# Gathering the attention products of a tile into one place of the matmul stream, in two PSUM banks used in turn, in a hybrid attention and pooling block

## The chip, the cores and the metric

The kernel runs on one core of one Trainium2 chip. The metric is device time in microseconds (us) of one execution, as the median of several runs. PE is TensorE, DVE is VectorE, ACT is ScalarE, POOL is GpSimd and SP is the sync engine, whose queue issues all DMAs here.

## The reference

One decoder block on x of 2048 x 1024 in fp32, with a final RMSNorm. What matters here is the attention: three groups of 8 heads of 64, with windows 128, 512 and 2048 and dilations 1, 4 and 16. Their outputs are joined by a softmax over the groups' log-denominators.

```python
proj = h @ w_in[l]                      # (2048, 8192): q, k, v of 3 groups, then gates and pooling
for gi, (win, dil) in enumerate(ATTN_GROUPS):
    o, lse = dilated_window_attention(qkv[:, :, gi, 0], qkv[:, :, gi, 1], qkv[:, :, gi, 2], dil, win // dil, bias_g)
    outs.append(o); lses.append(lse)
wts = jax.nn.softmax(jnp.stack(lses, axis=0), axis=0)
attn = jnp.sum(wts[..., None] * jnp.stack(outs, axis=0), axis=0)
y_attn = (attn * jax.nn.silu(z_attn)) @ w_attn_br[l]
```

A query attends to the 129 keys of its window (the queries' own block of 128 and the block before it). The pooling branch, the gates and the output projection follow.

## The kernel before, in words

The sequence is worked in two halves `h` of 1024 positions. In each half the projections run first in 12 units: four head pairs `hp` times three groups `g`, in the order 1, 2, 0. A unit (`unit`, L531) projects K, Q and V of one head pair, each in 8 main steps. A main step (`mm3`, L245) is six matmuls of 128x512: high and low parts of weights and activations, three products, two halves. So a unit has 24 main steps. Weights are split into a high part by VectorE (L217) and a low part by GpSimd (L218), six buffers deep.

The attention of one unit is a generator (`attention`, L545) that runs beside the main steps of the next unit: `weave` (L130) takes the main generator step by step and after each step advances the attention as often as keeps it even, `n_side` advances over `n_main - skip` steps. The last attention of a half runs beside the four pooling projections, 32 main steps (L976). PE and SP carry out their instructions in the order in which the program writes them (the manual schedule of L965); the other three engines are ordered by the scheduler.

One attention has 8 tiles of 128 queries. For a tile `t`:

- `prefetch` (L556): for tiles at the edge of the second half, DMAs of the keys of the first half and of this tile's keys into `khist`, and of the values into `vhist`.
- `logits` (L589): six matmuls with 64 rows into two banks `qk`; VectorE adds the bias and takes the minimum (L616), ScalarE takes the exponential (L620), VectorE adds the two blocks and takes a dot product with the identity (L629, L631).
- `transposed` (L638): two transposes into the bank `tp`; ScalarE copies them to `pT` (L646). For a tile with 256 keys GpSimd then multiplies and subtracts (L649, L650).
- `output` (L655): two or four matmuls into the bank `ops` (each is two in the trace); VectorE writes the row (L669 or L672). Groups 1 and 2 store it, group 0 reads the stored rows of the others and weighs all three (L683 to L701).
- `joined` (L703), group 0 only: one transpose of the joined row into `tp`; ScalarE copies it to `attnT` (L706).
- `flip` (L573), twice per attention: four transposes of V into `tp`, copied by ScalarE to `v` (L579).

PSUM has eight banks: four for the projections, two `qk`, one `tp`, one `ops`. Every one of the pieces above ends with a `yield`, so that a main step can stand between any two of them. The loop that sets their order is the end of `attention`:

```python
for s in range(12):
    if s < 8:
        prefetch(s + 2); logits(s); yield
    if s < 2:
        flip(s); yield
    if 1 <= s < 9:
        transposed(s - 1); yield
    if 2 <= s < 10:
        output(s - 2); yield
    if g == 0 and 4 <= s:
        joined(s - 4); yield
```

## Time and profile before

| what | value |
|---|---|
| median of 3 runs (lowest to highest) | 2363.19 us (2361.03 to 2369.22) |
| profiled execution, and its span | 2364.48 us, 2362.6 us |
| PE busy with matmuls | 2207.8 us (93%) in 11786 instructions |
| VectorE, ScalarE, GpSimd busy | 46%, 25%, 41% of the span |
| six products of the projections L253 (6000 matmuls, three groups) | 675.8 + 627.0 + 623.9 us |
| chain that ended last, by engine | PE 18%, no other over 2% |

The span is what the profiler saw of the program; the execution's own time is 1.9 us longer. A group of rows names a line, an engine, the tile written and the tiles read, the count, the busy time and the mean of one. A wait is given with the engine and line that released it. The granted clock is 1.00 for PE at 2.4 GHz and 0.50 at 1.2 GHz. Matmuls overlap: the time one takes of PE is read from start to start, not from its own length.

### The profile page before, as it was taken

Reading aid. Unit: us, or ns where it says so; the run is one execution under the profiler, and the core shown is the slowest. Engines: PE = TensorE matmul, PEld = TensorE weight load, DVE = VectorE, ACT = ScalarE, POOL = GpSimd, SP = SyncE. Lnnn points to the kernel's source line nnn. Section 1 sums busy time; section 2 is a strip of 40 time slices with the busy share of each in tenths; the row PEclk is TensorE's granted clock in tenths of the full one; section 3 lists DMA queues with packets and bytes.
Section 4 is the critical chain, followed back from the end, with each engine's and each line's share of the span. In section 5 each row is a group of like instructions: output and inputs, shape, how many; then the busy total and the mean of one; then the engine's idle time right before and its main releaser. Section 6 shows DMA issues by size and latency. Waiting matters only on the chain. (4 is left out here: it accounts for less than half of the span.)

```text
span 2362.6 us, 32338 instructions
## 1 busy us (share of the span) xinstructions
PE 2207.8 (93%) x11786; PEld 1802.4 (76%) x11786; DVE 1081.4 (46%) x3048; ACT 596.7 (25%) x1554; POOL 966.2 (41%) x930
## 2 busy tenths in 40 slices
PE   4799999999999999999899989999999899999998
PEld 3577777777777888888877767767777678888898
DVE  5444536336367211115764475564664861111155
ACT  4223232233332101102433333223322320010023
POOL 3322323213245223446754344344443552244365
PEclk7899999999999999999999999999999999999999
DMA  7243222222221112114432322222223111121134
GB/s 261 97 145 90 73 68 64 81 61 70 82 64 47 45 54 72 55 53 152 170 103 74 99 69 71 85 72 85 66 80 91 54 54 45 49 86 45 54 125 152
DMA packets 142685, 198.56 MB, mean 84 GB/s; under 512 B 13542, under 2 KB 109983, under 8 KB 142528
## 3 DMA queue, kind: packets, MB, share of 16 engines
q1 hardware_dynamic: 142528, 196.51, 26.2%
q8 instruction: 93, 1.52, 0.3%
q14 instruction: 64, 0.52, 0.1%
HBM read 157.62 MB, written 35.16 MB: 82 GB/s over the span
## 5 line engine op out<-in xcount | busy, mean ns | idle before, releaser
L218 POOL TENSOR_TENSOR wlo<-wraw,whi 128x512 fp32r<-128x512 f32 x352 | 470.7, 1340 | 848.9 <-PE mm L253 410.9
L253 PE MATMUL mm<-hhi,whi 128*128 128x512 f32 x2000 | 675.8, 419 | 2.0 <-DVE klo L509 2.0
L253 PE MATMUL mm<-hlo,whi 128*128 128x512 f32 x2000 | 627.0, 395 | 0.0
L253 PE MATMUL mm<-hhi,wlo 128*128 128x512 f32 x2000 | 623.9, 393 | 0.0
L217 DVE CAST whi<-wraw 128x512 fp32r<-128x512 f32 x352 | 197.5, 566 | 582.2 <-PE mm L253 411.4
L253 PEld LDWEIGHTS mm<-hhi,wlo 128*128 128x128 f32 x2000 | 378.3, 189 | 86.1
L253 PEld LDWEIGHTS mm<-hlo,whi 128*128 128x128 f32 x2000 | 378.3, 189 | 85.0
L253 PEld LDWEIGHTS mm<-hhi,whi 128*128 128x128 f32 x2000 | 338.6, 191 | 56.5 <-issue 3.0
L620 ACT ACTIVATE l<-l,row 128x256 f32<-128x256 f32 (+1 forms) x384 | 181.4, 474 | 493.1 <-DVE row L616 362.4
L616 DVE CUSTOM_DVE_ANT_0 l<-qk,bias 128x256 f32<-128x256 f32 (+1 forms) x384 | 133.7, 383 | 297.5 <-PE qk L613 275.3
L649 POOL TENSOR_TENSOR pT<-pT,prevm 128x256 f32<-128x256 f32 x140 | 100.2, 716 | 267.5 <-ACT pT L646 266.2
L734 ACT ACTIVATE sg<-mm 128x1024 f32<-128x1024 f32 x48 | 49.4, 1028 | 554.9 <-PE mm L253 422.5
L663 PEld LDWEIGHTS ops<-v,pT 128*128 128x128 f32 x1120 | 154.8, 191 | 26.5 <-POOL pT L650 11.4
L663 PE MATMUL ops<-v,pT 128*128 128x64 f32 x1120 | 155.2, 266 | 9.3 <-POOL pT L650 8.0
L917 PE MATMUL mm<-whi,mhi 128*128 128x256 f32 x512 | 149.3, 292 | 6.1 <-DVE yt L931 3.3
L917 PE MATMUL mm<-whi,mlo 128*128 128x256 f32 x512 | 146.7, 287 | 2.7 <-POOL mlo L741 2.7
L917 PE MATMUL mm<-wlo,mhi 128*128 128x256 f32 x512 | 146.4, 286 | 0.0
L631 DVE CUSTOM_DVE_ANT_0 dot<-l,ident 128x128 bf16<-128x128 f32 x216 | 108.8, 504 | 20.6 <-ACT l L620 20.6
L650 POOL TENSOR_TENSOR pT<-pT 128x256 f32<-128x256 f32 x140 | 110.8, 791 | 10.3
L646 ACT COPY pT<-tp 128x256 f32<-128x256 f32 x192 | 70.5, 367 | 172.7 <-PE tp L644 170.8
L917 PEld LDWEIGHTS mm<-whi,mhi 128*128 128x128 f32 x512 | 99.7, 195 | 7.0 <-DVE yt L931 3.6
L644 PE MATMUL tp<-ident,l 128*128 128x128 f32 x384 | 78.0, 285 | 27.4 <-ACT v L579 25.4
(182 smaller groups left out, 2680.5 us busy)
## 6 DMA issues: line engine op xcount, KB each, us to landing
wraw<-in_wpk_dram SPq DMA_DIRECT2D x176, 512.0 KB, 3.8
rows<-row SPq DMA_DIRECT2D x128, 66.0 KB, 1.7
row<-rows SPq DMA_DIRECT2D x64, 132.0 KB, 2.3
x<-in_x_dram SPq DMA_DIRECT2D x16, 512.0 KB, 4.8
wada<-in_w_ada_dram SPq DMA_DIRECT2D x32, 256.0 KB, 5.5
y<-in_x_dram SPq DMA_DIRECT2D x16, 512.0 KB, 7.5
out_dram<-yo SPq DMA_DIRECT2D x16, 512.0 KB, 6.4
khist<-kh SPq DMA_DIRECT2D x52, 128.0 KB, 2.5
```

Source lines behind the costliest of these rows:

```text
L217: copy(out=hi, in_=raw)
L218: nc.gpsimd.tensor_tensor(out=lo, in0=raw, in1=hi.bitcast(F32), op=ALU.subtract)
L253: nc.tensor.matmul(ps[:, n * 512:(n + 1) * 512], lhsT=w, rhs=m[:, n * 512:(n + 1) * 512], start=(k == 0 and j == 0), stop=(k == nk - 1 and ...
L616: nc.vector.tensor_tensor_reduce(out=l[:, i, :nk], in0=qks[i][:, :nk], in1=bt[:, i, 256 - nk:], scale=-1.0, scalar=1e38, op0=ALU.add, op1= ...
L620: nc.scalar.activation(out=l[:, i, :nk], in_=l[:, i, :nk], func=AF.Exp, scale=-1.0, bias=nm[:, i:i + 1], accum_out=rw[:, 130 + i:131 + i])
L631: nc.vector.tensor_tensor_reduce(out=junk, in0=prev[:, i, :], in1=ident, scale=1.0, scalar=0.0, op0=ALU.mult, op1=ALU.add, accum_out=d["fa ...
L644: nc.tensor.transpose(pps[:, i, :], d["l"][:, i, nk - P:nk], ident)
L646: nc.scalar.copy(out=pT[:, 1], in_=pps)
L649: nc.gpsimd.tensor_tensor(out=pT[:, 0], in0=pT[:, 1], in1=m, op=ALU.mult)
L650: nc.gpsimd.tensor_tensor(out=pT[:, 1], in0=pT[:, 1], in1=pT[:, 0], op=ALU.subtract)
L663: nc.tensor.matmul(ops[:, hs], lhsT=d["pT"][:, b, i, :], rhs=vv[:, hs], start=(b == 1), stop=(b == 0 or not full))
L917: nc.tensor.matmul(pst[:, pos:pos + 256], lhsT=st, rhs=mv, start=(fresh and i == 0), stop=(last and i == 2))
```

## The change

The pieces of a tile are gathered into one place between two main steps, a knot. Knot `s` takes one of two banks, writes the transposes of tile s-2 into its columns 0 to 255, the outputs of tile s-3 into 256 to 383, and, in group 0, the joined row of tile s-5 into 384 to 511, then the logits of tile s into the `qk` banks. Only after these matmuls are the copies and the row's work of the other engines written. The first two knots hold logits and a flip instead. There is one `yield` a knot, 11 knots for groups 1 and 2 and 13 for group 0; the generator is started once when it is made, before the next unit's first main step. The DMA of `vhist` leaves `prefetch` for `prefetch_v`, one tile ahead instead of two. The pools `ps_t` and `ps_o` with one bank each become `ps_k` with two.

```diff
-    ps_t = ctx.enter_context(tc.tile_pool(name="ps_t", bufs=1, space=PSUM))
-    ps_o = ctx.enter_context(tc.tile_pool(name="ps_o", bufs=1, space=PSUM))
+    ps_k = ctx.enter_context(tc.tile_pool(name="ps_k", bufs=2, space=PSUM))
...
     def tp():
-        return ps_t.tile([P, 512], F32, name="tp", tag="tp")
+        return ps_k.tile([P, 512], F32, name="knot", tag="knot")
...
-                d["prev"] = att.tile([P, P], F32, name="vhist", tag="vhist", bufs=4)
+
+        def prefetch_v(t):
+            if t >= 8:
+                return
+            d = st[t]
+            d["prev"] = None
+            if h == 1 and edge(t):
+                ht = {0: 0, 1: t % 4, 2: t}[g]
+                d["prev"] = att.tile([P, P], F32, name="vhist", tag="vhist", bufs=5)
                 nc.sync.dma_start(out=d["prev"], in_=vh[g][hp][ht])
...
-                d["row3"] = sm.tile([P, 3, RW], F32, name="row3", tag="row3", bufs=5)
+                d["row3"] = sm.tile([P, 3, RW], F32, name="row3", tag="row3", bufs=6)
...
-        def transposed(t):
+        def transposed(t, bank):
...
-            pps = tp()[:, :256].rearrange("p (i q) -> p i q", i=2)
+            pps = bank[:, :256].rearrange("p (i q) -> p i q", i=2)
             for i in range(2):
                 nc.tensor.transpose(pps[:, i, :], d["l"][:, i, nk - P:nk], ident)
+            yield
...
-        def output(t):
+        def output(t, bank):
             d = st[t]
-            ops = ps_o.tile([P, 512], F32, name="ops", tag="ops")
+            ops = bank[:, 256:384]
...
-        def joined(t):
-            aps = tp() if t < 7 else ps_o.tile([P, 512], F32, name="ops", tag="ops")
-            nc.tensor.transpose(aps[:, :P], st[t]["row3"][:, 0, 0:P], ident)
-            nc.scalar.copy(out=attnT[:, t * P:(t + 1) * P], in_=aps[:, :P])
+        def joined(t, bank):
+            aps = bank[:, 384:]
+            nc.tensor.transpose(aps, st[t]["row3"][:, 0, 0:P], ident)
+            yield
+            nc.scalar.copy(out=attnT[:, t * P:(t + 1) * P], in_=aps)
...
         prefetch(0)
         prefetch(1)
+        prefetch_v(0)
         yield
...
+        for s in range(13 if g == 0 else 11):
+            prefetch(s + 2)
+            prefetch_v(s + 1)
+            if s >= 2:
+                bank = tp()
+                parts_ = []
+                if s < 10:
+                    parts_.append(transposed(s - 2, bank))
+                if 3 <= s < 11:
+                    parts_.append(output(s - 3, bank))
+                if g == 0 and 5 <= s:
+                    parts_.append(joined(s - 5, bank))
+                for p in parts_:
+                    next(p)
+                if s < 8:
+                    logits(s)
+                for p in parts_:
+                    next(p, None)
+            else:
                 logits(s)
...
                 flip(s)
...
+            yield
...
                 queue = attention(h, g, hp, res)
-                n_queue = 28 if g else 36
+                next(queue)
+                n_queue = 11 if g else 13
...
-        weave(pool_in(h, hparts, pooled, todo), 32, queue, n_queue)
+        weave(pool_in(h, hparts, pooled, todo), 32, queue, n_queue, 1)
```

How the order on the engines moves, at three places of the built programs. The first is PE in the middle of an attention of group 0 of the first half; `mm` are main steps, `l` the probabilities, `row` the joined row. Before:

```order
L644 MATMUL tp<-ident,l 128x128 x2
L663 MATMUL ops<-v_1646,pT 128x64 x4
L253 MATMUL mm<-hhi_455,whi 128x512 x2
L253 MATMUL mm<-hlo_456,whi 128x512 x2
L253 MATMUL mm<-hhi_455,wlo 128x512 x2
L705 MATMUL tp<-ident,row_1728 128x128
L613 MATMUL qk<-khi_1338,qhi_1495 128x256 x2
L613 MATMUL qk<-khi_1338,qlo_1496 128x256 x2
L613 MATMUL qk<-klo_1339,qhi_1495 128x256 x2
L253 MATMUL mm<-hhi_470,whi 128x512 x2
L253 MATMUL mm<-hlo_471,whi 128x512 x2
L253 MATMUL mm<-hhi_470,wlo 128x512 x2
```

and in the changed program:

```order
L650 MATMUL knot<-ident,l 128x128 x2
L670 MATMUL knot<-v_1609,pT 128x64 x4
L713 MATMUL knot<-ident,row_1715 128x128
L619 MATMUL qk<-khi_1323,qhi_1495 128x256 x2
L619 MATMUL qk<-khi_1323,qlo_1496 128x256 x2
L619 MATMUL qk<-klo_1324,qhi_1495 128x256 x2
L252 MATMUL mm<-hhi_452,whi 128x512 x2
L252 MATMUL mm<-hlo_453,whi 128x512 x2
L252 MATMUL mm<-hhi_452,wlo 128x512 x2
L650 MATMUL knot<-ident,l 128x128 x2
L670 MATMUL knot<-v_1609,pT 128x64 x4
L713 MATMUL knot<-ident,row_1766 128x128
```

Transposes, outputs, joined row and logits, which stood in two places with a main step between them, stand in one, and the next knot follows one or two main steps later.

The second place is PE at the beginning of the same attention, at the second flip (`knot<-ident,vT` or `tp<-ident,vT`). Before:

```order
L613 MATMUL qk<-khi_1338,qhi_1495 128x256 x2
L613 MATMUL qk<-khi_1338,qlo_1496 128x256 x2
L613 MATMUL qk<-klo_1339,qhi_1495 128x256 x2
L253 MATMUL mm<-hhi_581,whi 128x512 x2
L253 MATMUL mm<-hlo_582,whi 128x512 x2
L253 MATMUL mm<-hhi_581,wlo 128x512 x2
L578 MATMUL tp<-ident,vT_1623 128x128 x4
L644 MATMUL tp<-ident,l 128x128 x2
L253 MATMUL mm<-hhi_590,whi 128x512 x2
```

and now:

```order
L619 MATMUL qk<-khi_1323,qhi_1495 128x256 x2
L619 MATMUL qk<-khi_1323,qlo_1496 128x256 x2
L619 MATMUL qk<-klo_1324,qhi_1495 128x256 x2
L584 MATMUL knot<-ident,vT_1607 128x128 x4
L252 MATMUL mm<-hhi_587,whi 128x512 x2
L252 MATMUL mm<-hlo_588,whi 128x512 x2
L252 MATMUL mm<-hhi_587,wlo 128x512 x2
L252 MATMUL mm<-hhi_650,whi 128x512 x2
L252 MATMUL mm<-hlo_651,whi 128x512 x2
L252 MATMUL mm<-hhi_650,wlo 128x512 x2
L650 MATMUL knot<-ident,l 128x128 x2
```

The first transposes of probabilities, which stood right behind the second flip in the same bank, stand two main steps behind it.

The third place is ScalarE in the same attention, with the buffer numbers and the semaphores that each row waits for (PE_49 is PE's, DVE_49 VectorE's, Pool_49 GpSimd's). Before:

```order
L522 ACTIVATE qhi109_3538<-mm_3290 128x1024 [waits PE_49]
L646 COPY pT_3511<-tp_3508 128x256 [waits PE_49,Pool_49]
L690 ACTIVATE e_3659<-e_3659 128x6 [waits DVE_49]
L706 COPY attnT106_3126<-tp_3557 128x128 [waits PE_49]
L620 ACTIVATE l_3562,row3_3560<-l_3562,row3_3560 128x256 [waits DMAHW3_49,DVE_49,Activation_49]
L620 ACTIVATE l_3562,row3_3560<-l_3562,row3_3560 128x256 [waits DVE_49]
L646 COPY pT_3589<-tp_3586 128x256 [waits PE_49,Pool_49]
L690 ACTIVATE e_3689<-e_3689 128x6 [waits DVE_49]
L706 COPY attnT106_3126<-tp_3622 128x128 [waits PE_49]
```

and now:

```order
L521 ACTIVATE qhi109_3509<-mm_3199 128x1024 [waits PE_49]
L653 COPY pT_3486<-knot_3458 128x256 [waits PE_49,Pool_49]
L698 ACTIVATE e_3589<-e_3589 128x6 [waits DVE_49]
L626 ACTIVATE l_3468,row3_3466<-l_3468,row3_3466 128x256 [waits DMAHW2_49,DVE_49,Activation_49]
L626 ACTIVATE l_3468,row3_3466<-l_3468,row3_3466 128x256 [waits DVE_49]
L715 COPY attnT106_3062<-knot_3458 128x128 [waits DVE_49]
L653 COPY pT_3536<-knot_3528 128x256 [waits PE_49,Pool_49]
L715 COPY attnT106_3062<-knot_3528 128x128 [waits DVE_49]
```

The copy of the joined row, which waited for PE, waits for VectorE, that is for the row's reading of the same bank; the copy of `pT` of knot 3458 now waits for the last matmul of its knot, where that of `tp_3508` waited for its own transposes.

## Rows read from the trace of the kernel before

**Rows 1.** PE's waits, whole span: who <- whom, line: us in total, times, longest.

```profile
PE tp L644 <- ACT v L579: 25.4, 23, 3.6
PE qk L613 <- DMA khist<-khi: 20.9, 12, 2.6
PE tp L705 <- ACT pT L646: 18.1, 16, 2.1
...
PE qk L613 <- DVE row L616: 14.1, 1, 14.1
...
PE ops L663 <- POOL pT L650: 8.0, 8, 1.2
...
PE ops L705 <- DVE row L701: 3.3, 2, 1.9
```

**Rows 2.** Stretches of 100 us: length, busy us (instructions) by engine, granted clock, DMA.

```profile
200.00:300.00 100.00, 93.24 (x513) 72.39 (x512) 56.39 (x214) 31.01 (x101) 33.49 (x37) 0.98 0.25 72
...
800.00:900.00 100.00, 100.00 (x442) 82.78 (x442) 16.59 (x32) 6.17 (x6) 23.23 (x18) 1.00 0.15 48
...
1800.00:1900.00 100.00, 92.65 (x508) 72.10 (x508) 70.99 (x219) 30.00 (x90) 50.51 (x50) 0.98 0.23 68
```

**Rows 3.** Timeline of PE, pool stage: start us, us, line, tile, count.

```profile
700.78 1.00 PE L663 MATMUL ops<-v,pT 128*128 128x64 f32 x8
701.59 0.70 PE L253 MATMUL mm<-hhi,whi 128*128 128x512 f32 x2
...
703.06 0.27 PE L705 MATMUL tp<-ident,row 128*128 128x128 f32 x1
703.09 0.71 PE L253 MATMUL mm<-hhi,whi 128*128 128x512 f32 x2
...
704.64 0.39 PE L613 MATMUL qk<-khi,qhi 64*128 64x256 f32 x2
...
705.20 0.73 PE L253 MATMUL mm<-hhi,whi 128*128 128x512 f32 x2
...
706.70 0.38 PE L644 MATMUL tp<-ident,l 128*128 128x128 f32 x2
706.83 0.71 PE L253 MATMUL mm<-hhi,whi 128*128 128x512 f32 x2
...
708.30 1.00 PE L663 MATMUL ops<-v,pT 128*128 128x64 f32 x8
```

**Rows 4.** Timeline of SP (queue of DMA issues), start of a unit of h = 1.

```profile
1296.96 0.56 SPq L564 DMA_DIRECT2D khist<-kh  x1
```

**Rows 5.** Timelines of PE, ACT, POOL: one tile's chain with nothing in front.

```profile
1451.53 0.38 PE L644 MATMUL tp<-ident,l 128*128 128x128 f32 x2
...
1452.01 0.37 ACT L646 COPY pT<-tp 128x256 f32<-128x256 f32 x1 [2.53 <-PE tp L644]
...
1453.21 0.72 POOL L650 TENSOR_TENSOR pT<-pT 128x256 f32<-128x256 f32 x1
```

**Rows 6.** Timelines of PE, ACT, POOL: one tile's chain with other work in front.

```profile
246.56 0.38 PE L644 MATMUL tp<-ident,l 128*128 128x128 f32 x2
246.78 1.00 PE L663 MATMUL ops<-v,pT 128*128 128x64 f32 x8
...
247.61 0.51 ACT L620 ACTIVATE l<-l,row 128x256 f32<-128x256 f32 x1 [2.84 <-issue]
...
249.52 0.35 ACT L646 COPY pT<-tp 128x256 f32<-128x256 f32 x1
...
248.54 1.29 POOL L218 TENSOR_TENSOR wlo<-wraw,whi 128x512 fp32r<-128x512 f32 x1 [1.83 <-DVE whi L217]
...
251.69 0.75 POOL L650 TENSOR_TENSOR pT<-pT 128x256 f32<-128x256 f32 x1
```

**Rows 7.** Short stretches around one long wait of PE; columns as in rows 2.

```profile
217.00:220.00 3.00, 0.82 (x6) 0.48 (x4) 2.50 (x17) 1.87 (x7) 0.26 (x1) 1.00 0.13 43
...
222.00:224.00 2.00, 2.00 (x10) 1.59 (x10) 0.94 (x5) 0.53 (x3) 0.00 (x0) 0.50 0.00 0
```

More of the change, by code (lines that the diff above doesn't have):

```diff
@@ L328, in bank @@
             return ps_qk.tile([P, 512], F32, name="hp", tag="qk")
-        return tp() if i % 4 == 2 else ps_o.tile([P, 512], F32, name="ops", tag="ops")
+        return tp()
     def transposed_x(tiles, p0, hp_):
@@ L559, in prefetch @@
             d = st[t]
-            d["prev"] = None
             if h == 1 and edge(t):
@@ L671, in output @@
             else:
-                nc.vector.tensor_copy(out=rw[:, 0:P], in_=ops[:, :P])
+                nc.vector.tensor_copy(out=rw[:, 0:P], in_=ops)
             if g:
@@ L701, in output @@
             nc.vector.tensor_tensor(out=row[:, 0, 0:P], in0=row[:, 0, 0:P], in1=row[:, 2, 0:P], op=ALU.add)
-        def joined(t):
-            aps = tp() if t < 7 else ps_o.tile([P, 512], F32, name="ops", tag="ops")
-            nc.tensor.transpose(aps[:, :P], st[t]["row3"][:, 0, 0:P], ident)
-            nc.scalar.copy(out=attnT[:, t * P:(t + 1) * P], in_=aps[:, :P])
+        def joined(t, bank):
[3 more added lines that the diff above has]
+            nc.scalar.copy(out=attnT[:, t * P:(t + 1) * P], in_=aps)
         prefetch(0)
         prefetch(1)
+        prefetch_v(0)
         yield
-        for s in range(12):
-            if s < 8:
-                prefetch(s + 2)
+        for s in range(13 if g == 0 else 11):
[17 more added lines that the diff above has]
+            else:
                 logits(s)
-                yield
-            if s < 2:
                 flip(s)
-                yield
-            if 1 <= s < 9:
-                transposed(s - 1)
-                yield
-            if 2 <= s < 10:
-                output(s - 2)
-                yield
-            if g == 0 and 4 <= s:
-                joined(s - 4)
-                yield
+            yield
         if g == 0:
```

## The prediction

> **What bounds the kernel now.** I read the stretches of 100 us first, then PE's waits, then timelines of single tiles. In a stretch of nothing but projections PE is busy all of the time: 442 matmuls in 100 us, so a main step of six takes 6 x 100 / 442 = 1.357 us [rows 2]. In the two stretches with attention that are shown PE is busy 93 of 100 us, VectorE 56 and 71, GpSimd 33 and 51 [rows 2]. So PE bounds both, and what attention costs is PE's time twice over: the time of its small matmuls, and the time in which PE, taking its queue in order, stands before one of them.
>
> The waits have few causes [rows 1]. 25.4 us in 23 waits are transposes of a tile's probabilities that stand right behind the second flip of V and need the one `tp` bank, which ScalarE is still copying. 18.1 us in 16 waits are joined rows that need the same bank while ScalarE copies the probabilities. 20.9 us in 12 waits are the first logits of a unit of the second half, which wait for the history keys. 8.0 us are outputs that wait for GpSimd to finish pT, and 3.3 us joined rows that wait for VectorE.
>
> The small matmuls cost more than they take, because the main step behind them starts slowly. In one round [rows 3]: outputs 701.59 - 700.78 = 0.81, the step behind them 1.47 instead of 1.357, so 0.92 in all; a joined row 0.03 and a step of 1.55, 0.22; logits 0.56 and 1.50, 0.70; transposes 0.13 and 1.47, 0.24. Together 2.08 us a round.
>
> **The change, part by part.** Below, T, O, J, L and F are transposes, outputs, joined rows, logits and flip.
>
> *Two banks in turn.* In the built order a flip and the next transposes now lie in different knots and different banks, with two main steps between: the 25.4 us go. J writes into the bank that T has just written, and waits for no copy: the 18.1 us go. A knot waits instead for the readers of the knot two before, some 9 us earlier; I cost that at nothing.
>
> *History keys.* The change asks for them when the unit is created. On SP's queue their DMAs now stand ahead of a weight load and of the last row store of the unit before. In the old order they stand behind both: the first was issued at 1296.96 in the unit shown [rows 4]. The first logits come after four main steps instead of three (three in group 0, four in the pool stage). One or two row stores and a step are 1.4 to 3 us; the mean wait is 20.9 / 12 = 1.7 and the longest 2.6 [rows 1]. I take all 20.9 away. vhist goes behind the keys on SP, with four knots until its output: nothing.
>
> *The end of group 0.* O and J of the last tile are two knots apart, three steps: the 3.3 us go.
>
> *Fewer interruptions.* Counted in the two built orders, attention breaks into the main stream in 555 places before and 290 after. What does a merged place save? T right ahead of O takes 246.78 - 246.56 = 0.22 [rows 6], against 0.24 alone: 0.02. At most it saves the whole slow step, 1.47 - 1.357 = 0.11. Nearest are pieces side by side, so I take 0.05, near the lower end: 265 x 0.05 = 13 us, between 5 and 29.
>
> *The new wait.* This is where the change can lose. In the built program ScalarE's copy of T's result waits for the last matmul in that bank, so for O and J of the same knot; VectorE's reading of O waits for that copy, and ScalarE's copy of J for VectorE. Before, the copy waited for T alone. So there is a ring: O of one tile, the copy of the next tile's T, two GpSimd operations, then O of that next tile, one knot later. With nothing in front, from T's end (1451.53 + 0.38) to the end of GpSimd's second operation (1453.21 + 0.72), it takes 2.0 us [rows 5]. With two exponentials and a copy of Q in front on ScalarE (247.61 to 249.52, about 1.0 us each) and a weight split (1.29) in front on GpSimd, it took 251.69 + 0.75 - 246.94 = 5.5 us [rows 6]. What is there for it? Ahead of L 1.55 - 1.47 = 0.08, L 0.56, its slow step 0.14, two steps 2.71, the next T 0.22 [rows 3, 6]: 3.7 us. Where only one step lies between (two places in each of the eight units of group 0), 2.36.
>
> In the built order ScalarE's copy now stands ahead of the exponentials of its knot in nearly every knot, while the weight split still stands ahead of GpSimd's pair at about every second knot: 2.0 + 1.3 = 3.3 us, below 3.7. With a copy of K, Q or V as well, about 1 us more, a knot waits 0.6; one of the three per unit is badly placed, 24 x 0.6 = 14 us. The 16 places with one step: 0.4 each, 6 us. I take 20 us, in place of the 8.0 of before. The bounds: nothing, and 140 full tiles x (5.5 - 3.7) = 252 us.
>
> Sharing a bank among readers is what a rule speaks against. The Trainium skill, PSUM — Partial Sum Buffer, section "PSUM bank collisions raise a hardware error", says that two engines may not touch one bank at once, even in different columns, and that one guards by bank, not by address. No row of before shows it, for there a bank holds one result. Were each copy behind its own matmuls alone, O and J (0.84 us [rows 3]) would drop out of the ring, the 20 us would be near nothing, and the sum 2263.
>
> *The clock.* PE's clock is at half, 1.2 of 2.4 GHz, for a short time after a long wait: in 217 to 220 PE is busy 0.82 of 3 us, and 222 to 224 runs at 0.50 [rows 7]. Seven of the stretches of 100 us with attention stand at 0.97 or 0.98, the first and last are shown [rows 2]: 2 us each, some 15 in all, part of it in PE's idle time. With the waits gone I take 11 us off.
>
> **The sum.** 25.4 + 18.1 + 20.9 + 3.3 + 8.0 + 13 + 11 = 99.7 us less, 20 us more: 79.7. The profiled execution took 2364.48 us (2362.6 of span), so 2284.8; the median of the runs lies 1.3 lower: 2283.5, **2283 us**. An engine that could take PE's place as the bound is far off: VectorE is 71% busy in the fuller stretch [rows 2].
>
> **Rivals.**
> *The ring decides (slower).* If the copies fall behind the exponentials after all, 2.0 + 1.0 + 1.3 = 4.3 us is the least with a split in front, and 5.5 the most [rows 6]; midway, 4.9, each of 140 full tiles waits 1.2, 168 us, and the 16 short places 1.36 more, 22. Then 2364.5 - 99.7 + 190 - 1.3 = 2454 us. It makes the kernel slower from a mean wait of 99.7 / 140 = 0.71 us a tile on. For it: the eight such waits of before, with a longer way from T to O [rows 1]. Against: the built order.
> *The ring takes half.* Every second tile waits 4.3 - 3.7 = 0.6, and the short places 1.36 more: 42 + 22 = 64 us in place of 20, 2327 us.
> *The clock falls in the knots (slower).* A knot is about 1.9 us of small matmuls. If PE's clock fell after one knot in three, 67 of some 200, at 2 us each: 134 us more, and the 11 not gained: 2283 + 145 = 2428 us. The Trainium skill, TensorE: Matmul & The Clock Gate, section "A second HAM failure mode: psum-queue depth-cycling", tells of a kernel that cycled PSUM banks, idled briefly between groups of matmuls and so swung between the two clocks; by that rule this case would be likely. The rows are against it: the fall shown follows an idle PE, and a knot without a wait has no idle time.
> *The waits come back.* The next lock takes them: the two banks for the old one, the khist wait as before. Without 25.4, 18.1, 20.9 and the 11 of the clock, 2283 + 75 = 2358 us, as good as no change.
>
> **How the numbers follow.** 0.3% is 7 us, about what a measurement of this kernel can tell from no change. Chances: forecast (2255 to 2300) 0.62, half ring 0.18, waits back 0.09, ring 0.07, clock 0.04. Faster: 0.62 + 0.18 and a third of 0.09, 0.83; same 0.06; slower 0.11. Below, with the whole 29 us of merging, no new wait and all 15 us of the clock, it would be about 2283 - 16 - 20 - 4 = 2243; I go to 2252, near that end. Above, to 2335, past the half ring; some 0.2 is left out.
>
> **What would show it.** In the profile after, PE's waits should lack `tp` on ScalarE's copy of V, joined rows on the copy of pT, and logits on khist. A new row, outputs on GpSimd's pT, should hold 10 to 30 us; over 100 us there is the ring. Attention stretches should stand at a granted clock of 1.00; below 0.95 there, the knots cost the clock. The copy of pT should start behind O, not behind T. If PE's waits fall by less than 50 us, the sum is wrong in its first terms; if they fall and the time does not, in the merging.

## The result, and the profile after

The changed kernel takes 2271.2 us (median of 4 runs, 2269.5 to 2274.3), the kernel before 2362.8 in the runs beside it: a ratio of 0.9609, 95% interval [0.9588, 0.9631]. It is 91.6 us faster; the forecast was 2283 us, and the range held. The profiled execution has a span of 2272.5 us, 90.1 less than before.

The head of the page of the changed kernel:

```profile
span 2272.5 us, 32250 instructions
PE 2174.9 (96%) x11786; PEld 1816.6 (80%) x11786; DVE 1011.5 (45%) x3048; ACT 599.3 (26%) x1554; POOL 942.3 (41%) x930
```

The waits of PE in the changed kernel, as in [rows 1]:

```profile
PE knot L670 <- POOL pT L657: 22.7, 14, 4.5
...
PE qk L619 <- DVE row L622: 13.0, 1, 13.0
```

The rows of transposes on ScalarE's copy of V, of joined rows on its copy of pT and on VectorE, and of logits on khist are gone. The row of outputs on GpSimd's pT has grown from 8.0 to 22.7 us, and the one long wait of the first unit (14.1 before, 13.0 now) has nothing to do with the change.

Where did the 90 us go? Two parts of the span, one in each half, hold attention beside projections. Each is taken from the third main step of the unit beside which the first attention runs, which stands in front of the first logits in both kernels, to the first matmul of the pooled products in half 0 and to the first final projection in half 1, so that the matmuls in it are the same. Columns as in [rows 2]. The kernel before:

```profile
92.98:745.19 652.21, 604.22 (x3274) 471.83 (x3272) 329.62 (x1182) 191.97 (x610) 206.94 (x213) 0.97 0.27 81
1243.57:2259.45 1015.88, 968.55 (x4989) 775.23 (x4988) 462.52 (x1450) 240.36 (x647) 418.28 (x423) 0.99 0.23 69
sum 1668.09, PE 1572.77 PEld 1247.06 DVE 792.14 ACT 432.33 POOL 625.21; mean PE 786.38 PEld 623.53 DVE 396.07 ACT 216.17 POOL 312.61
```

The changed kernel, in the same two parts:

```profile
94.27:705.40 611.13, 586.17 (x3273) 478.68 (x3272) 303.24 (x1182) 192.75 (x610) 195.64 (x213) 0.98 0.28 87
1203.92:2170.14 966.22, 954.42 (x4989) 784.16 (x4988) 417.43 (x1450) 242.22 (x647) 406.05 (x423) 0.99 0.24 72
sum 1577.35, PE 1540.59 PEld 1262.84 DVE 720.66 ACT 434.98 POOL 601.69; mean PE 770.30 PEld 631.42 DVE 360.33 ACT 217.49 POOL 300.84
```

The two parts are 1668.09 - 1577.35 = 90.7 us shorter: all of the gain, and nothing was lost elsewhere. PE's idle time in them fell from 1668.09 - 1572.77 = 95.3 to 36.8 us, so 58.6 us of the gain are waits that went. The other 32 us are PE's own busy time, for the same matmuls. Over a third of the gain is in no row of waits.

Three of the stretches of 100 us, as in [rows 2]:

```profile
200.00:300.00 100.00, 98.80 (x564) 80.81 (x564) 55.71 (x235) 33.83 (x107) 37.65 (x46) 1.00 0.28 82
...
600.00:700.00 100.00, 91.84 (x492) 74.89 (x491) 69.59 (x226) 30.42 (x90) 40.57 (x37) 0.97 0.19 54
...
800.00:900.00 100.00, 100.00 (x443) 82.81 (x442) 17.00 (x31) 8.26 (x8) 30.89 (x22) 1.00 0.19 63
```

The first is what most of attention looks like now (eight of the thirteen stretches from 100 to 700 and from 1200 to 1900 stand at 1.00, five before): 564 matmuls where 513 stood, PE busy 98.8 of 100 us, the clock at 1.00. The second is the pool stage of half 0, where waits are left. Nothing but projections (the third) runs as before.

One round of the changed kernel in group 0, in the timeline of PE (start us, us, engine, line, tile), to set beside [rows 3]:

```profile
227.69 0.38 PE L650 MATMUL knot<-ident,l 128*128 128x128 f32 x2
227.91 1.00 PE L670 MATMUL knot<-v,pT 128*128 128x64 f32 x8
228.75 0.28 PE L713 MATMUL knot<-ident,row 128*128 128x128 f32 x1
228.96 0.39 PE L619 MATMUL qk<-khi,qhi 64*128 64x256 f32 x2
...
229.51 0.74 PE L252 MATMUL mm<-hhi,whi 128*128 128x512 f32 x2
...
231.02 0.63 PE L252 MATMUL mm<-hhi,whi 128*128 128x512 f32 x2
...
232.41 0.38 PE L650 MATMUL knot<-ident,l 128*128 128x128 f32 x2
```

The knot takes 229.51 - 227.69 = 1.82 us, the step behind it 1.51 and the next 1.39 in place of 1.357. Together a round costs 1.82 + 0.15 + 0.03 = 2.00 us, against 2.08 for the four separate pieces of before.

### The profile page after: what moved, and what is told of

Its sections match the earlier page's. It is cut to its first block, busy times and chain, and to the rows that moved or that the text cites. A ratio compares the mean times of both kernels' runs of the same rounds, so it can differ in the third digit from the quotient of the medians.

```text
span 2272.5 us, 32250 instructions
## 1 busy us (share of the span) xinstructions
PE 2174.9 (96%) x11786; PEld 1816.6 (80%) x11786; DVE 1011.5 (45%) x3048; ACT 599.3 (26%) x1554; POOL 942.3 (41%) x930
## 5 line engine op out<-in xcount | busy, mean ns | idle before, releaser
L252 PE MATMUL mm<-hhi,whi 128*128 128x512 f32 x2000 | 650.8, 407 | 2.0 <-DVE klo L508 2.0
L252 PEld LDWEIGHTS mm<-hhi,whi 128*128 128x128 f32 x2000 | 356.4, 189 | 79.3 <-issue 2.9
L670 PE MATMUL knot<-v,pT 128*128 128x64 f32 x1120 | 157.9, 269 | 22.7 <-POOL pT L657 22.7
L670 PEld LDWEIGHTS knot<-v,pT 128*128 128x128 f32 x1120 | 147.5, 193 | 28.3 <-POOL pT L657 26.3
L653 ACT COPY pT<-knot 128x256 f32<-128x256 f32 x192 | 71.2, 371 | 241.2 <-PE knot L670 220.1
L933 PEld LDWEIGHTS mm<-whi,mlo 128*128 128x128 f32 x512 | 99.7, 195 | 3.5 <-POOL mlo L757 3.5
L933 PEld LDWEIGHTS mm<-wlo,mhi 128*128 128x128 f32 x512 | 99.8, 195 | 0.1
```

What stands on the lines that cost most here:

```text
L252: nc.tensor.matmul(ps[:, n * 512:(n + 1) * 512], lhsT=w, rhs=m[:, n * 512:(n + 1) * 512], start=(k == 0 and j == 0), stop=(k == nk - 1 and ...
L653: nc.scalar.copy(out=pT[:, 1], in_=pps)
L670: nc.tensor.matmul(ops[:, hs], lhsT=d["pT"][:, b, i, :], rhs=vv[:, hs], start=(b == 1), stop=(b == 0 or not full))
L933: nc.tensor.matmul(pst[:, pos:pos + 256], lhsT=st, rhs=mv, start=(fresh and i == 0), stop=(last and i == 2))
```

## The experiments

The theory after the result: the gain is a sum of separate parts, namely the keys asked for early, the waits for ScalarE's copies, the interruptions, and the clock; what is left of waits is the ring that the prediction described. The rivals are named with each run.

### The keys alone

In the kernel before, the first piece of a unit's attention is taken when the generator is made; the other pieces keep their places.

```diff
...
-                    weave(mixed(main, gates) if hp or g == GORDER[-1] else main, 24, queue, n_queue, 1)
+                    weave(mixed(main, gates) if hp or g == GORDER[-1] else main, 24, queue, n_queue, 1, 1)
                     run(queue)
                 queue = attention(h, g, hp, res)
+                next(queue)
...
```

(The last argument lets weave count one piece as done.)

> The kernel before, with one thing of the change alone: the first piece of each attention generator, which issues the two key-history loads and the first two value loads, is taken when the generator is made, a projection earlier; every other piece keeps its place among the steps. Theory (the gain is a sum of separate causes): the wait of the first logits for khist (20.9 us in 12 places) goes, and nothing else; the waits for ACT's copies (25.4 and 18.1 us) stay as they are: about 2362.8 - 21 = 2342 us, and 1 or 2 us less if a fall of the clock goes with it (2338 to 2345). Rival (the loads take longer when they run beside the end of the former unit's transfers, so the wait moves to another place): no gain, 2358 to 2366 us, and a new wait of the logits or of the value differences.

Measured: 2334.9 us, ratio 0.9878 [0.9861, 0.9894] to 2363.3. The khist row is gone and the rows on ScalarE's copies stand, 25.6 and 18.7 us. The gain, 28.4 us, is 7.5 more than the row; the granted clock gives the likely rest: over the thirteen stretches of 100 us from 100 to 700 and from 1200 to 1900, the hundredths missing from 1.00 add up to 27 us before and to 15 us here (some of them in idle time).

### Two banks alone

In the kernel before, one pool of two banks in turn serves flips, transposes, outputs and joined rows; the pieces stay where they were.

```diff
-    ps_t = ctx.enter_context(tc.tile_pool(name="ps_t", bufs=1, space=PSUM))
-    ps_o = ctx.enter_context(tc.tile_pool(name="ps_o", bufs=1, space=PSUM))
+    ps_t = ctx.enter_context(tc.tile_pool(name="ps_t", bufs=2, space=PSUM))
...
-            ops = ps_o.tile([P, 512], F32, name="ops", tag="ops")
+            ops = tp()
...
-            aps = tp() if t < 7 else ps_o.tile([P, 512], F32, name="ops", tag="ops")
+            aps = tp()
```

> The kernel before with its one bank for transposes and its one bank for outputs made one pool of two banks, taken in turn by every flip, transpose, output and joined row; the order of the pieces stays as it was. Theory (in the change it is the place of the transposes, ahead of outputs of an older tile and two steps behind the flips, that took the waits for ACT away): two banks in turn only pass the wait on, because outputs now take their turn in the same pair and are read out by DVE or GpSimd: of the 43.5 us of waits for ACT's copies a half or less goes, and new waits on readers of the outputs take part of it back: 2335 to 2365 us. Rival (the second bank alone takes the waits away): all 43.5 us go, about 2319 us or less, with no row of transposes waiting for ACT left.

Measured: 2326.1 us, ratio 0.9841 [0.9826, 0.9856]. Neither side had it whole. The waits of PE:

```profile
PE qk L612 <- DMA khist<-khi: 20.7, 12, 2.6
PE tp L704 <- ACT pT L645: 19.7, 17, 2.1
...
PE tp L662 <- POOL pT L649: 7.9, 8, 1.2
```

All 25.4 us of transposes on ScalarE's copy of V went, with the transposes still right behind the flip: the second bank is enough for them. None of the joined rows' wait went: with three pieces a round and two banks, the joined row comes back to the bank of its round's transposes. New waits come to some 5 us. The gain, 37.2 us, is 11.8 more than the row that went; the hundredths missing from the granted clock fell from 27 to 13 us over the same thirteen stretches.

### Both together

> The kernel before with both of the parts that were tried alone: the first keys requested a projection earlier, and two banks in turn for transposes, outputs and flips; the pieces stay scattered over the steps and keep their order. Theory (the parts are separate): the two differences add up, 28.4 + 37.2 us below 2363.3, so 2298 us (2293 to 2302), and the 26 us that stay between it and the changed kernel are the joined rows' wait for ACT's copy (19.7 us, still there) and the interruptions that only the knots take away, less the waits that the knots add. Rival (one of the parts worked through the clock that the other also restores): the sum falls short by 8 us or more, 2305 us and above.

The edit is that of the two runs above. Measured: 2298.9 us, ratio 0.9722 [0.9704, 0.9739]: 65.3 us below its 2364.2 of before, where the parts give 65.6. They add up. What stays to the changed kernel, 27.7 us, is the knots' own. The same two parts show what is in it:

```profile
94.43:718.98 624.55, 595.25 (x3274) 468.50 (x3272) 327.89 (x1182) 190.03 (x610) 207.21 (x213) 0.98 0.28 84
1216.30:2192.44 976.14, 958.43 (x4990) 770.79 (x4988) 463.00 (x1450) 238.86 (x647) 417.96 (x423) 1.00 0.24 72
sum 1600.69, PE 1553.68 PEld 1239.29 DVE 790.89 ACT 428.89 POOL 625.17; mean PE 776.84 PEld 619.65 DVE 395.45 ACT 214.44 POOL 312.59
```

Idle time is 47.0 us, 10 more than in the changed kernel, and busy time 13.1 us more, with 11 us missing from the clock's 1.00 here (same thirteen stretches) and 18 in the changed kernel. So the knots save some 13 to 20 us of PE's busy time. The other half reads against before: with every interruption in place, busy time fell by 1572.77 - 1553.68 = 19.1 us, of which the clock explains at most 27 - 11 = 16. Some 3 us or more went with 35 waits, beyond their idle time. That is one trace, and the keys alone show no such rest: there busy time fell by 10 us, and the clock's share is up to 12.

### One bank for the knots

```diff
-    ps_k = ctx.enter_context(tc.tile_pool(name="ps_k", bufs=2, space=PSUM))
+    ps_k = ctx.enter_context(tc.tile_pool(name="ps_k", bufs=1, space=PSUM))
```

(in the changed kernel)

> The changed kernel with one bank for all knots in place of two. Theory (the distance of the knots in the matmul stream, two steps in most places, does the work, and the second bank covers only the 16 one-step places of group 0 in each half, the ends of the halves and the flips): 20 to 40 us slower than the changed kernel, 2291 to 2311 us, with the new waits at the first transpose of a knot in group 0 and near none in groups 1 and 2. Rival (the two banks are what removed the waits of before): the first matmul of every knot waits for the last reader of the one before, 100 us or more are lost, 2370 us and above.

Measured: 2281.2 us, ratio 0.9654 [0.9639, 0.9668], 10 us over the changed kernel, less than the theory's 20. The waits of PE:

```profile
PE knot L336 <- ACT hraw L341: 12.4, 6, 4.7
...
PE knot L650 <- ACT attnT L715: 10.0, 15, 1.0
PE knot L670 <- POOL pT L657: 6.4, 5, 3.7
PE knot L650 <- ACT v L585: 4.0, 5, 1.4
```

The first row has nothing to do with attention: line 336 transposes the normed input, and its six waits lie between 1110 and 1172 us, where half 1 is made ready. In attention 10.0 and 4.0 us of new waits stand against 16.3 us less on pT; in the same two parts PE's idle time is 37.6 us, against 36.8, and the parts are 3.4 us longer. So in the new order the second bank is worth at most some 3 us to attention, and in the old order (the run with two banks alone) it was worth the 25.4 us. The order and the bank are two cures for one wait.

### The keys late

The changed kernel without its early `next(queue)`; the pieces are then 12 and 14 a unit.

```diff
-                next(queue)
-                n_queue = 11 if g else 13
+                n_queue = 12 if g else 14
```

> The changed kernel with its attention generators' first piece, which requests the key history, taken within the weave as before, and not when the generator is made; knots and banks stay as changed. Theory (the early request is a part of its own, worth in the kernel before 20.9 us of waits and some 7 us of clock): the khist row comes back with 12 places and about 20 us, and the time is 2290 to 2300 us. Rival (in the knots the first logits stand with the first flip and come later than before, so that the load is hidden anyway): no khist row, 2268 to 2275 us.

Measured: 2309.4 us, ratio 0.9763 [0.9745, 0.9781]: 38 us slower than the changed kernel, and neither side was right. There is no khist row at all. The pieces are fewer and stand further apart than before, and that is enough for the load. What came instead:

```profile
PE knot L670 <- POOL pT L657: 38.5, 36, 2.9
```

With 12 pieces on 23 main steps the last knot of each unit stands one step behind the one before, in groups 1 and 2 too. 11 pieces go in at every second step exactly (main steps 3, 5, ... 23, counted from 0). So what the early request is worth in the change is, as far as this run shows, a piece that is no longer woven in; the time of the request and the number of pieces changed together here. The pT row explains 16 of the 38 us, the clock 5 (23 missing us against 18); the rest was not taken apart.

### The new wait: bank or queue?

The changed kernel with transposes in a bank of their own, outputs and joined row in the other:

```diff
-    ps_k = ctx.enter_context(tc.tile_pool(name="ps_k", bufs=2, space=PSUM))
+    ps_k = ctx.enter_context(tc.tile_pool(name="ps_k", bufs=1, space=PSUM))
+    ps_o = ctx.enter_context(tc.tile_pool(name="ps_o", bufs=1, space=PSUM))
...
-                bank = tp()
...
-                    parts_.append(transposed(s - 2, bank))
+                    parts_.append(transposed(s - 2, tp()))
+                bank = op() if s >= 3 else None
```

> The changed kernel with its two banks divided by use and not by turn: the transposes of a knot always go to one, its outputs and joined row to the other, so ACT's copy of the transposes no longer stands behind the outputs and joined row of its own knot. Theory (the 22.7 us that outputs now wait for GpSimd's pT are the chain that runs through the shared bank, longer by the outputs and the joined row, 0.84 us): that row falls to about 10 us, and if no other wait comes the time is 2258 to 2266 us. Rival 1 (the wait is that of GpSimd's and DVE's load, not of the bank): the row stays between 18 and 25 us and the time within 4 us of 2271. Rival 2 (with one bank each, outputs wait for the readers of the last knot's outputs): the row falls, but a new one of outputs or transposes on DVE or ACT of more than 12 us stands in its place, 2271 to 2295 us.

Measured: 2269.6 us (2267.1 to 2274.9), ratio 0.9605 [0.9587, 0.9623]: not told apart from the changed kernel.

```profile
PE ops L674 <- POOL pT L661: 15.5, 11, 2.7
...
PE ops L717 <- ACT attnT L719: 2.0, 1, 2.0
PE ops L674 <- ACT attnT L719: 1.4, 2, 1.1
PE knot L654 <- ACT pT L657: 1.2, 1, 1.2
```

Rival 1 has the time, and none the row: it fell by 7 us, and 4.6 came back beside it. Why the bank matters so little is in the timelines of the changed kernel, around the first of its 14 waits. ScalarE, GpSimd, PE:

```profile
232.84 1.02 ACT L521 ACTIVATE qhi<-mm 128x1024 fp32r<-128x1024 f32 x1
233.84 0.37 ACT L653 COPY pT<-knot 128x256 f32<-128x256 f32 x1
...
234.54 1.30 POOL L217 TENSOR_TENSOR wlo<-wraw,whi 128x512 fp32r<-128x512 f32 x1 [1.85 <-DVE whi L216]
235.81 0.66 POOL L656 TENSOR_TENSOR pT<-pT,prevm 128x256 f32<-128x256 f32 x1
236.54 0.73 POOL L657 TENSOR_TENSOR pT<-pT 128x256 f32<-128x256 f32 x1
...
237.32 1.10 PE L670 MATMUL knot<-v,pT 128*128 128x64 f32 x8 [1.20 <-POOL pT L657]
```

The copy has landed at 234.21 and GpSimd is idle, but its queue has a weight split next, which waits for VectorE until 234.54; the two operations on pT stand behind it. And the copy itself began when ScalarE had made the high part of Q, at 233.84, when the outputs and the joined row in its bank were also just done. In 10 of the 14 waits a split stood in front on GpSimd when the copy landed: it was running in three, and in seven, as here, it still waited for VectorE. In the other 4 the copy was late, behind an exponential of the joined rows that waited for VectorE:

```profile
1325.71 0.21 ACT L698 ACTIVATE e<-e 128x6 f32<-128x6 f32 x1 [0.97 <-DVE e L697]
1325.82 0.36 ACT L653 COPY pT<-knot 128x256 f32<-128x256 f32 x1
```

Here the joined row of the bank had started at 1322.77. All 14 waits are in attentions of group 0. Five of them, 6.6 us, stand where the knot is one main step behind the last. Three, 3.8 us, stand two steps behind it, with the copy late. The other six, 12.4 us, are in the two pool stages, where the last attention of each half runs (the same row in the windows 640:700 and 1760:1810):

```profile
PE knot L670 <- POOL pT L657: 7.2, 3, 4.5
...
PE knot L670 <- POOL pT L657: 5.2, 3, 3.4
```

The forecast's places, the copies of K, Q and V in every unit, have none in groups 1 and 2. That the copy waits for the whole bank is true, and the timeline shows it where nothing else is in front:

```profile
238.64 0.37 ACT L653 COPY pT<-knot 128x256 f32<-128x256 f32 x1 [1.17 <-PE knot L713]
```

### One GpSimd operation in the chain

If the queue and the operations are the chain, a shorter chain must show. The outputs are computed from all of pT with the tile's own values, and from the masked part with the difference of the values.

```diff
+            if nk == 256:
+                vd = d["vd"] = att.tile([P, P], F32, name="vd", tag="vd", bufs=2)
+                nc.gpsimd.tensor_tensor(out=vd, in0=d["prev"], in1=vcur[t], op=ALU.subtract)
...
                 nc.gpsimd.tensor_tensor(out=pT[:, 0], in0=pT[:, 1], in1=m, op=ALU.mult)
-                nc.gpsimd.tensor_tensor(out=pT[:, 1], in0=pT[:, 1], in1=pT[:, 0], op=ALU.subtract)
-                if g < 2:
-                    vd = d["vd"] = att.tile([P, P], F32, name="vd", tag="vd", bufs=2)
-                    nc.gpsimd.tensor_tensor(out=vd, in0=d["prev"], in1=vcur[t], op=ALU.subtract)
...
-            vs = [(1, vcur[t])] + ([(0, d["prev"])] if full else [])
+            vs = [(1, vcur[t])] + ([(0, d["vd"])] if full else [])
```

> The changed kernel with one GpSimd operation on pT in place of two between ACT's copy and the outputs: the masked part is still multiplied out, but the other part is not made by a subtraction (0.73 us); the outputs multiply all of pT by the tile's own values and the masked part by the difference of the values, which GpSimd works out ahead. In 10 of the 14 waits of outputs for pT the trace shows GpSimd still in a split (of weights, 1.30 us, or of 2.4 us) when the copy had landed, in the other 4 ACT's copy itself late behind an exponential of the joined rows. Theory (the wait is the queue on GpSimd and ACT ahead of the chain, then the two operations): each place gets about 0.7 us shorter, the row falls from 22.7 to about 13 us and the time to 2258 to 2264 us. Rival (GpSimd's order moves with it, so that another operation takes the place of the subtraction): the row stays above 18 us and the time within 4 us of 2271.

Measured: **2255.4 us**, ratio 0.9537 [0.9520, 0.9554], 15.8 us below the changed kernel and the fastest of all.

```profile
PE knot L669 <- POOL pT L659: 10.8, 9, 3.2
```

The row lost 11.9 us where some 10 were expected, and the time is 3 us below the expected range; with the clock (12 us missing instead of 18) that is the gain. The edit also takes work off GpSimd, 515.1 us busy in the two parts where the changed kernel has 601.7, so the run does not tell a shorter chain from a shorter queue in front of it.

### The mask on VectorE

The same kernel, with the remaining operation taken from GpSimd:

```diff
-                nc.gpsimd.tensor_tensor(out=pT[:, 0], in0=pT[:, 1], in1=m, op=ALU.mult)
+                nc.vector.tensor_tensor(out=pT[:, 0], in0=pps, in1=m, op=ALU.mult)
```

> The kernel with one GpSimd operation on pT, with that operation given to VectorE, which multiplies the transposes by the mask straight out of the bank while ACT copies them: no GpSimd operation is left between transposes and outputs but the difference of the values, worked out ahead. Theory (what stays of the wait, 10.8 us, is mostly GpSimd held by a split of the weights): the pT row falls to 5 us or less and the time to 2246 to 2252 us. Rival 1 (VectorE's queue holds the multiplication as GpSimd's did): a row on VectorE or ACT of 8 us or more, 2253 to 2262 us. Rival 2 (VectorE's added load delays the splits of the weights and the exponentials that stand behind it): above 2262 us, with new waits of the projections or logits.

Measured: 2260.1 us, ratio 0.9569 [0.9556, 0.9582], 4.7 us above the kernel with one GpSimd operation. Rival 1 holds: the wait changed its owner, and 6.9 us came in which joined rows waited for nothing that the profile shows.

```profile
PE knot L669 <- DVE pT L659: 10.0, 10, 1.3
PE knot L712 <- issue: 6.9, 2, 3.5
```

VectorE's timeline at the first of these waits:

```profile
232.87 1.21 DVE L522 SCALAR_TENSOR_TENSOR qlo<-mm,qhi 128x1024 fp32r<-128x1024 f32 x1
234.01 0.41 DVE L622 CUSTOM_DVE_ANT_0 l<-qk,bias 128x256 f32<-128x256 f32 x1
...
234.69 0.41 DVE L659 TENSOR_TENSOR pT<-knot,prevm 128x256 f32<-128x256 f32 x1
```

The low part of Q and the reading of the knot's logits stand ahead. At these places each of the three engines has one long operation in its queue (ScalarE the high part of Q, VectorE its low part, GpSimd a weight split). Nor did VectorE multiply beside ScalarE's copy out of the same bank, as the expectation had it; in 73 places it waited for that copy:

```profile
DVE pT L659 <- ACT pT L656: 119.8, 73, 3.3
```

### The price of an interruption

First the logits in places of their own in every group:

```diff
                 for p in parts_:
                     next(p)
-                if s < 8:
-                    logits(s)
                 for p in parts_:
                     next(p, None)
+                if s < 8:
+                    yield
+                    logits(s)
...
-                n_queue = 11 if g else 13
+                n_queue = 17 if g else 19
```

> The changed kernel with the logits of a tile taken out of its knot and put in a place of their own between two knots: 6 more interruptions of the projections in each of the 24 units, 144 in all; outputs still follow their transposes one knot later, but 2.4 steps or more behind, since logits stand between. Theory (an interruption costs about 0.095 us, which is 25 us over the 265 that the change took away): 14 us for the interruptions, less some 10 us of waits for GpSimd's pT that the longer distance takes away: 2271 to 2280 us, and the pT row at 12 us or less. Rival (0.05 us each, as forecast): 7 us less the same waits: 2264 to 2270 us. Rival (joining the pieces is what most of the gain came from): 2290 us or more.

Measured: 2335.3 us, ratio 0.9874 [0.9857, 0.9891], 64 us slower than the changed kernel and far outside what the theory said. My expectation had overlooked the ends: behind the last logits the knots have no logits between them and stand one step apart.

```profile
PE knot L670 <- POOL pT L657: 44.4, 32, 6.2
```

This row (22 us more), other waits (some 6) and the clock (29 us missing over the thirteen stretches, 11 more than in the changed kernel) are 39 of the 64 us. Two things changed at once, so the run gives no price; it does show what badly spaced knots cost. The second try keeps the knots two steps apart with empty pieces, in groups 1 and 2 alone:

```diff
-                if s < 8:
+                if g == 0 and s < 8:
                     logits(s)
                 for p in parts_:
                     next(p, None)
+                if g and s < 10:
+                    yield
+                if g and s < 8:
+                    logits(s)
             else:
                 logits(s)
                 flip(s)
+                if g:
+                    yield
             yield
...
-                n_queue = 11 if g else 13
+                n_queue = 21 if g else 13
```

> The changed kernel with the logits of groups 1 and 2 taken out of the knot and put one step behind it, and the knots themselves kept two steps apart by empty pieces; group 0 stays as changed. It adds 6 interruptions in each of 16 units, 96 in all, without the crowded ends that the run with logits in places of their own had in all groups. Theory (an interruption costs 0.095 to 0.13 us: 25 us over 265 in the change, 18 over 144 in that run): 9 to 12 us slower than the changed kernel, 2279 to 2285 us, with the pT row within 3 us of 22.7. Rival 1 (0.05 us, as forecast): 2274 to 2278 us. Rival 2 (the separate places bring the half clock back, as in that run): 2286 us or more, with more stretches below a granted clock of 1.00 than the changed kernel has.

Measured: 2280.0 us, ratio 0.9657 [0.9644, 0.9670], 8.8 us slower than the changed kernel.

```profile
PE knot L670 <- POOL pT L657: 22.5, 15, 4.6
```

The waits are the same (22.5 against 22.7), the clock a little better (15 us missing against 18), and PE's busy time in the two parts is 1547.2 us against 1540.6:

```profile
sum 1585.09, PE 1547.20 PEld 1248.53 DVE 752.28 ACT 435.80 POOL 606.04; mean PE 773.60 PEld 624.27 DVE 376.14 ACT 217.90 POOL 303.02
```

For 95 places more in the trace, the 8.8 us between the medians are 0.093 us for one, or 0.12 with the clock's 3 us added. The busy time alone gives 6.6 us, 0.07 for one, or 0.10 with the clock. So the price lies between 0.07 and 0.12: near the theory's, and above 0.05.

## Why the prediction was right

The direction, the main terms and the time (2283 forecast, 2271 measured, 12 us apart) were right. Of waits, 75.7 us less the 20 new ones, so 55.7, were forecast to go, and 58.6 us of idle time went; of busy time, 13 + 11 = 24 us were forecast and 32 went. By its own steps:

- **Two banks in turn** (43.5 us): the size was right, both rows are gone. The reason was half the story. The wait behind the flips has two cures, each enough: the bank alone took it away in the old order, and with one bank in the new order 4.0 us of it are left. The joined rows' wait went with the order alone; two banks in the old order left 19.7 us.
- **History keys** (20.9 us): the row is gone, and asking early does it in the old order. In the new order the wider spacing does it as well; there the early request is worth 38 us, 16 of them for another reason, the outputs that wait where knots stand closer, which the prediction did not see; the rest of the 38 stays open but for some 5 us of clock.
- **The end of group 0** (3.3 us): gone.
- **Fewer interruptions** (13 us, between 5 and 29): too small. The direct test gives 0.07 to 0.12 us for a place in which logits stand apart. At its 0.093, taken for all 265 places, that is 25 us. The rounds give less: 0.08 us in the round shown, 15 us if all 192 tiles are like it, because transposes and joined rows were cheap where they stood. Against the scattered order with the same banks and keys the knots save 13 to 20 us of busy time. So some 13 to 25, where I took the lower end of the price.
- **The new wait** (20 us): 22.7 us, but mostly for the wrong places and by the wrong cause, so that the size came out is in large part luck. I put 14 us at copies of K, Q and V in all groups; there are none in groups 1 and 2, and 12.4 us stand in the pool stages instead, which had no term. I put 6 us at sixteen places one step apart, 0.4 each; the trace has twelve such places with outputs, since the attentions beside the pooling projections have none, and 6.6 us in five of them. And I made the shared bank the lock. A bank of its own for the transposes gained nothing that could be measured: a split on GpSimd or an exponential on ScalarE was in front anyway. One operation less in the chain, and less of GpSimd's work, gained 15.8 us. The copy that starts behind the joined row in its bank, 1.17 us of waiting in the row shown, agrees with the rule of the Trainium skill (PSUM — Partial Sum Buffer, section "PSUM bank collisions raise a hardware error"). But the sum without that lock, 2263, did not come: 2269.6.
- **The clock** (11 us): 9 at most, with 27 us missing in the thirteen stretches before and 18 after. Half of these 18 lie in the first stretch, 100 to 200, at the long wait of the first unit; the other half in the pool stages and at one wait of group 0, none in knots without a wait. The rival of a clock that falls after every third knot is out, since the stretch from 200 to 300, full of knots, stands at 1.00. The swing that the Trainium skill tells of (TensorE: Matmul & The Clock Gate, section "A second HAM failure mode: psum-queue depth-cycling") is in no stretch in which the knots follow without idle time.
- **What was missing**: PE's busy time fell by 32 us, and interruptions (13 to 20 against the scattered order) and the clock (9 at most) leave 3 us or more without a term. In the scattered order with two banks and early keys, where no interruption was saved, some 3 us beyond the clock went with 35 waits. One row hints at how: outputs that had waited take 1.10 us, others 1.00. That a wait costs more than its idle time and the clock is not shown, and the keys alone speak against it.

Of the signs that the prediction asked for, most held. The rows that should go are gone, the new row is between 10 and 30 us, the copy of pT starts behind the joined row of its bank, and waits fell by more than 50 us and the time with them. The sign of the clock held in part: eight of the thirteen stretches stand at 1.00, and none is below 0.95 but the first, 0.91.

## What to carry to other kernels

When small work is woven into a dense stream, look first at how far apart dependent pieces end up in the stream: with 12 pieces in place of 11 on the same steps, and the keys asked for later, the kernel was 38 us slower here, 16 of them in outputs that waited, in groups 1 and 2 because the last pieces then stand one step apart and not two. A wait that several engines share was shortened here by taking an operation out of its chain; another bank gained nothing measurable, and another engine only changed the wait's owner, while each queue held one long operation. And two changes that cure the same wait are not worth their sum: try each alone before giving it a share.

## What was not expected of the hardware

- A single piece of logits set apart from its knot costs about 0.09 us of PE's time (0.07 to 0.12) with no more waits and no more loss of clock. The step between a joined row and logits takes 1.55 us [rows 3], the first step behind logits 1.50, in the changed kernel 1.51, and behind outputs or transposes 1.47, in place of 1.357. Joining only transposes to outputs saves almost nothing (0.22 against 0.24 us).
- Where the granted clock fell goes with how long a wait was more than with how many there were. In the changed kernel it fell to 0.50 at three of the 14 waits for pT, those of 4.5, 1.75 and 3.4 us (below, stretches of 2 or 3 us that take in the end of each wait or lie behind it; columns as in [rows 2]). With the logits in places of their own it fell at each of the eight waits of this row of 3.0 to 6.2 us, and at none of the other 24 (0.7 us at most). With the keys alone 48 waits for the copies of V and pT and for GpSimd's pT are left, 3.1 us at the longest, and only 15 us of clock are missing, fewer than the 18 of the changed kernel with its 14.

```profile
674.00:677.00 3.00, 1.89 (x10) 1.89 (x10) 2.65 (x18) 0.42 (x2) 1.06 (x2) 0.50 0.00 0
...
1630.00:1632.00 2.00, 2.00 (x7) 1.52 (x6) 1.90 (x11) 0.61 (x3) 1.41 (x2) 0.50 0.64 188
...
1798.00:1801.00 3.00, 3.00 (x12) 2.81 (x13) 2.75 (x20) 0.79 (x3) 0.81 (x2) 0.50 0.02 5
```
